# A state space stage on GpSimd: shared first phases, copies moved to ScalarE, a feed-through and an input split moved to VectorE

## The chip, the cores and the metric

The kernel runs on one core of a Trainium2 chip. The core has a matrix engine (TensorE, in the profile PE, with its weight loads as PEld), VectorE (DVE), ScalarE (ACT), GpSimd (POOL) and SyncE (SP), which only issues DMAs. Each engine works through its own list of instructions in order; an instruction that waits holds all behind it on its engine. The metric is device time in microseconds for one execution of the whole program.

## The reference

Two trunk layers are computed for 1024 latent tokens and 128 context tokens (1152 columns in all), D = 1024. Layer 0 mixes tokens by a diagonal state space model (S5) and by differential attention; layer 1 by a short convolution and a gated recurrence. Each is followed by a gated convolutional FFN (D_FF = 2816). What matters here is the S5 part and the product into the second FFN:

```python
def s5_direction(u, lam_re, lam_im, log_dt, b_w, c_w, h0, reverse):
    ...
    ab_r, ab_i = mag * jnp.cos(ang), mag * jnp.sin(ang)
    ...
    if h0 is not None:
        br = br.at[:, 0].add(ab_r * h0r - ab_i * h0i)
        bi = bi.at[:, 0].add(ab_r * h0i + ab_i * h0r)
    _, _, hr, hi = lax.associative_scan(_cplx_comb, (ar, ai, br, bi), axis=1)
    final = jnp.stack([hr[:, -1], hi[:, -1]], axis=1)
    y = jnp.einsum('blgn,gpn->blgp', hr, c_w[0]) - jnp.einsum('blgn,gpn->blgp', hi, c_w[1])
    return y, final

# in mixer_ab: both directions, 32 groups of 16 channels and 64 states
ys = u4 * s5_d.reshape(S5_G, S5_P)          # the feed-through
ys = ys + y_d                                # for d in (forward, backward)
ys = jax.nn.gelu(ys.reshape(b, L, HALF))

def conv_ffn(h, w_up, cw, cb, w_down):
    u = dwconv(h @ w_up, cw, 1) + cb
    g, val = jnp.split(u, 2, axis=-1)
    return (jax.nn.gelu(g) * val) @ w_down
```

## The kernel before

Every large matrix product is done in three: each factor is split into a rounded part (`hi`, written by ScalarE) and the remainder (`lo`, a subtraction on VectorE or GpSimd), and hi·hi, hi·lo and lo·hi are added in PSUM.

**State space stage.** The sequence is cut in chunks of 8 tokens, 144 chunks with both token groups. The 32 groups are done in 8 blocks of 4 (`G_ = 4`); both directions sit in the upper and lower 64 partitions. `s5_params` first works out the parameters of all groups, almost all of it on VectorE; among them `Lr`, `Li`, the phase of one chunk squared 0 to 6 times. Then, for each block, `s5_prep` builds its tables and `s5_main` uses them. The table `E` holds the phases of 0 to 143 chunks, made by doubling: for `m` from 0 to 6 the first `n = 2**m` columns times phase `m` give the next `n`, in six GpSimd instructions (L619 to L621); the last 16 columns repeat the first 16 (L623). `s5_prep` also makes `ca` (GpSimd product `d`, VectorE sum, L655 and L656), the convolution kernel of a chunk (`kps` on TensorE, `ks`, with the feed-through `dd` added on its middle, L673 to L676, written to DRAM as `kt` and read back as `M`, both by DMAs on ScalarE's queue, L677 and L680), and the input matrix `W` (products `d` L685 to L687, transposed as `wps`). `s5_main` multiplies the inputs by `W` (`zps`), turns them by `E` (`x`), scans them on VectorE (`X`, L727 and L728), copies the last states out and the first states in (L731 to L737, GpSimd), turns them back (`s`, GpSimd L743 and VectorE L744 and L745), multiplies by `ca` and `M` (`yps`) and applies the gelu (L758). Table `b + 1` is prepared before block `b` is used. `s5_main` is emitted at higher priority.

**Order.** The instructions' order on each engine comes from a planner that simulates the program as written and lets later work (the projections for attention, `vps` and `pps`, and the modulation rows `mps`) fill time in which earlier work waits. It is fixed before the run.

**Second FFN.** Its up projection runs as a seven-product scheme on 2 by 2 blocks of inputs (`11`, `12`, `21`, `22`, `T1` to `T4`, four slices each of 576 columns). `T1` and `T2` are made as the tokens arrive (`Blocks.put`), the rest in `Blocks.rest`: for each input the rounded part on ScalarE and the remainder on the named engine (`split`, L107 and L108), `T3 = 22 - 12` (L115) and `T4 = 21 - T2` in two subtractions (L122 and L126). The function `after` chains these instructions so that each engine keeps the order in which they are written. The products themselves (`prod`, L1565, result `sps`) come in the order T2, T1, 11, 22, 21, T3, T4, and their weights are split by `pair` (`wp`, L1505 and L1506).

## Time and profile before

| | us |
|---|---|
| median of 3 runs | 2981.25 |
| lowest, highest | 2980.51, 2983.24 |
| the profiled execution | 2977.45 |
| its span, first to last instruction | 2975.7 |

| engine | busy us | share of the span |
|---|---|---|
| PE | 2779.2 | 93% |
| DVE | 2053.7 | 69% |
| ACT | 1136.2 | 38% |
| POOL | 955.6 | 32% |

Busy time is that of instructions on the engine; DMA issues and waits are not in it. The shares are means over stages that differ much. Durations further on come from the profiled execution, whose time stands beside its span above.

### The profile page before, as it was taken

What the parts mean: (1) busy time and instruction counts of PE and PEld (TensorE: products, weight loads), DVE (VectorE), ACT (ScalarE), POOL (GpSimd) and SP (SyncE); (2) the same over time, 40 slices, a digit from 0 to 9 for tenths busy, and PEclk for the clock granted to TensorE, in tenths of its full rate; (3) what the DMA queues carried; (4) which work ended last, traced back from release to release, by engine and by line L of the source; (5) the groups of instructions that cost most, each with busy time, mean ns of one, the idle gap of its engine ahead of it and who ended that gap; (6) DMA issues with size and microseconds to landing.
All of it is one profiled execution on the core that took longest, in us unless ns stands there. A gap on an engine that the chain in (4) does not pass through costs nothing.

```text
span 2975.7 us, 41289 instructions
## 1 busy us (share of the span) xinstructions
PE 2779.2 (93%) x15560; PEld 2504.5 (84%) x15560; DVE 2053.7 (69%) x3266; ACT 1136.2 (38%) x1916; POOL 955.6 (32%) x1047
## 2 busy tenths in 40 slices
PE   7977687998999999999999989999979999998998
PEld 3875566787789999999999979997769999997887
DVE  6767784876468888888655684456488888884224
ACT  5222122776353222222222365564544444443211
POOL 2699972012130000000000251111166666653100
PEclk9988898999999999999999989999979999999999
DMA  6424447334543332333111231124312222225323
GB/s 224 130 64 111 112 132 225 111 98 122 161 141 100 93 100 81 98 100 95 48 43 57 71 116 55 54 94 132 110 46 72 70 84 69 69 96 168 93 61 123
DMA packets 315653, 299.68 MB, mean 101 GB/s; under 512 B 46334, under 2 KB 272338, under 8 KB 315454
## 3 DMA queue, kind: packets, MB, share of 16 engines
q1 hardware_dynamic: 293544, 261.00, 28.5%
q0 software_dynamic: 4496, 20.91, 2.1%
q10 hardware_dynamic: 17414, 15.14, 1.9%
q8 instruction: 122, 2.00, 0.3%
q14 instruction: 77, 0.63, 0.1%
HBM read 230.68 MB, written 66.30 MB: 100 GB/s over the span
## 4 chain that ended last, share of the span: by engine, by line
PE 63%; issue 3%; DVE 2%; POOL 2%; ACT 1%; DMA 0%; ACTq 0%; POOLq 0%; DVEq 0%; SPq 0%
PE pps L189 27%; PE sps L1565 16%; PE dps L189 8%; PE dps L1682 8%; PE ops L189 3%; PE gps L189 1%; POOL hl L54 1%; DVE l L108 0%; DVE yl L1398 0%; POOL rs L239 0%; PE tps L377 0%; POOL tf L115 0%; PE mps L334 0%; PE mps L333 0%; POOL q L239 0%
## 5 line engine op out<-in xcount | busy, mean ns | idle before, releaser
L189 PE MATMUL pps<-hl,whi 128*128 128x384 f32 (+1 forms) x1824 | 624.2, 342 | 1.5 <-DVE hl L886 0.8
L189 PE MATMUL pps<-hh,whi 128*128 128x384 f32 (+1 forms) x1824 | 624.5, 343 | 0.3 <-DVE lruc L1342 0.3
L189 PE MATMUL pps<-hh,wlo 128*128 128x384 f32 (+1 forms) x1824 | 622.4, 342 | 2.3 <-DVE wlo L201 2.3
L189 PEld LDWEIGHTS pps<-hh,whi 128*128 128x128 f32 x1824 | 346.7, 190 | 10.2 <-issue 3.9
L189 PEld LDWEIGHTS pps<-hh,wlo 128*128 128x128 f32 x1824 | 346.6, 190 | 8.5 <-DVE wlo L201 3.2
L189 PEld LDWEIGHTS pps<-hl,whi 128*128 128x128 f32 x1824 | 346.6, 190 | 7.7 <-DVE hl L886 1.6
L201 POOL TENSOR_TENSOR wlo<-wr,whi 128x1024 fp32r<-128x1024 f32 x22 | 57.0, 2603 | 737.8 <-PE dps L189 595.2
L1682 PE MATMUL dps<-wp,wp 128*128 128x512 f32 x1188 | 279.5, 397 | 8.0 <-DVE C L1523 5.9
L1682 PEld LDWEIGHTS dps<-wp,wp 128*128 128x128 f32 x1188 | 225.4, 190 | 62.0 <-ACT cc L1642 6.1
L1639 DVE SCALAR_TENSOR_TENSOR cc<-C,cvc,cc 128x1023 f32<-128x1023 f32 (+1 forms) x176 | 225.8, 1322 | 35.1 <-ACT cc L1634 35.1
L1565 PE MATMUL sps<-h,wp 128*128 128x288 f32 x1056 | 188.7, 298 | 10.7 <-DVE wp L1506 9.4
L1436 DVE SCALAR_TENSOR_TENSOR cc<-pps,cvc,cc 128x384 f32<-128x384 f32 (+2 forms) x352 | 171.1, 509 | 39.8 <-ACT cc L1433 37.7
L326 DVE SCALAR_TENSOR_TENSOR macc<-mw,sil,macc 128x256 f32<-128x256 f32 x392 | 176.1, 484 | 17.9 <-DMA mw<-w_mod 17.1
L1482 DVE TENSOR_TENSOR acc<-acc,dps 128x512 f32<-128x512 f32 x180 | 122.4, 680 | 76.3 <-PE dps L189 75.7
L1565 PEld LDWEIGHTS sps<-h,wp 128*128 128x128 f32 x1056 | 157.8, 190 | 11.2 <-DVE wp L1506 9.6
L199 ACT ACTIVATE whi<-wr 128x1024 fp32r<-128x1024 f32 x102 | 107.5, 1056 | 153.9 <-PE pps L189 101.7
L189 PE MATMUL dps<-whi,mh 128*128 128x512 f32 x396 | 156.9, 397 | 1.2 <-DVE acc L1482 1.2
L189 PE MATMUL dps<-wlo,mh 128*128 128x512 f32 x396 | 156.6, 396 | 0.0
L189 PE MATMUL dps<-whi,ml 128*128 128x512 f32 x396 | 155.6, 393 | 0.0
L1433 ACT ACTIVATE cc<-pps,cvc 128x385 f32<-128x385 f32 (+1 forms) x132 | 87.4, 665 | 173.9 <-PE pps L189 160.9
L201 DVE TENSOR_TENSOR wlo<-wr,whi 128x1024 fp32r<-128x1024 f32 x80 | 101.8, 1274 | 70.8 <-PE pps L189 36.2
L1523 POOL TENSOR_TENSOR C<-U,X 128x576 f32<-128x576 f32 x44 | 105.4, 2396 | 134.2 <-DVE U L1523 134.2
(423 smaller groups left out, 6033.5 us busy)
## 6 DMA issues: line engine op xcount, KB each, us to landing
mw<-w_mod SPq DMA_DIRECT2D x224, 128.0 KB
x<-x SPq DMA_DIRECT2D x45, 512.0 KB
wr<-ffn_w_up SPq DMA_DIRECT2D x44, 512.0 KB
wr<-ffn_w_down SPq DMA_DIRECT2D x44, 512.0 KB
wm<-w_mod SPq DMA_DIRECT2D x40, 512.0 KB
m<-cc SPq DMA_DIRECT2D x21, 576.0 KB
k<-kh POOLq DMA_DIRECT2D x8, 1408.0 KB, 6.7
wv<-ffn_w_up SPq DMA_DIRECT2D x21, 512.0 KB
```

The lines of the kernel that those rows point to most:

```text
L54: nc.gpsimd.tensor_tensor(lv, h, f(hv), op=OP.subtract)
L189: nc.tensor.matmul(ps, x, y, start=first and i == 0 and j == 0, stop=last and i == n - 1 and j == 2)
L199: nc.scalar.activation(hi, raw, AF.Copy)
L201: (eng or nc.vector).tensor_tensor(lo, raw, f(hi), op=OP.subtract)
L326: nc.vector.scalar_tensor_tensor(acc[v], wt, s, acc[v], op0=OP.mult, op1=OP.add)
L1433: nc.scalar.activation(cc[:, :no], ps[:, q:q + no], AF.Identity, bias=cw[3], scale=cw[1])
L1436: nc.vector.scalar_tensor_tensor(cc[:, oa - o0:ob - o0], ps[:, oa + d - i0:ob + d - i0], cw[j], cc[:, oa - o0:ob - o0], op0=OP.mult, op1=O ...
L1482: nc.vector.tensor_tensor(acc[t][:, sl], acc[t][:, sl], ps, op=OP.add)
L1523: tt = lambda e, o, x, y, op: e.tensor_tensor(o, x, y, op=op)
L1565: nc.tensor.matmul(ps[:, c, :W2], w, z[:, c * W2:c * W2 + W2], start=m == 0, stop=m == len(steps) - 1)
L1639: nc.vector.scalar_tensor_tensor(cc[:, o0:o1], src[:, o0 + d:o1 + d], cw[j], cc[:, o0:o1], op0=OP.mult, op1=OP.add)
L1682: nc.tensor.matmul(ps[:, h], mt[:, x, i], W[fb][:, y, h * 512:h * 512 + 512], start=i == 0 and j == 0, stop=i == n - 1 and j == 2)
```

## The change

The first three doublings of `E` (columns 0 to 7) are computed for all 32 groups at once, in `s5_params`, into two tables `EP`; each block copies its part from there on ScalarE and goes on with `m = 3`. The copy of the last 16 columns of `E`, and the four state copies of each scan, go from GpSimd to ScalarE; the two memsets between them stay on GpSimd. The feed-through `dd` on GpSimd and its addition on VectorE become one fused instruction on VectorE for each group. `h0` is kept in a rotating buffer in place of a constant one. In `Blocks.rest` the differences for `T3` and the remainders of `T3` go from GpSimd to VectorE, the `T3` split is put ahead of `T4`, and `T4` is worked slice by slice: both subtractions, the rounding, the remainder.

```diff
@@ Blocks.rest
         for i in range(4):
-            after(G.tensor_tensor(t3[i], raw["22"][i], raw["12"][i], op=OP.subtract))
+            after(V.tensor_tensor(t3[i], raw["22"][i], raw["12"][i], op=OP.subtract))
...
+        self.hi["T3"], self.lo["T3"] = new("T3h"), new("T3l")
+        split("T3", t3, V)
         t4 = temp()
+        self.hi["T4"], self.lo["T4"] = new("T4h"), new("T4l")
         for i in range(4):
             after(V.tensor_tensor(t4[i], raw["21"][i], f(self.hi["T2"][:, i]), op=OP.subtract))
-        self.hi["T3"], self.lo["T3"] = new("T3h"), new("T3l")
-        split("T3", t3, G)
-        for i in range(4):
             after(V.tensor_tensor(t4[i], t4[i], f(self.lo["T2"][:, i]), op=OP.subtract))
-        self.hi["T4"], self.lo["T4"] = new("T4h"), new("T4l")
-        split("T4", t4, V)
+            after(A.activation(self.hi["T4"][:, i], t4[i], AF.Copy))
+            after(V.tensor_tensor(self.lo["T4"][:, i], t4[i], f(self.hi["T4"][:, i]), op=OP.subtract))
@@ s5_params
+        G = nc.gpsimd
+        self.EP = [C([128, 32, 8], f"EP{x}") for x in range(2)]
+        G.memset(self.EP[0][:, :, 0:1], 1.0)
+        G.memset(self.EP[1][:, :, 0:1], 0.0)
+        for m in range(3):
+            n = 1 << m
+            lr, li = (x[:, m, :, None].to_broadcast([128, 32, n]) for x in (self.Lr, self.Li))
+            e0, e1 = (e[:, :, 0:n] for e in self.EP)
+            for o, x0, x1, op in ((0, lr, li, OP.subtract), (1, li, lr, OP.add)):
+                t0, t1 = self.tp([128, 32, n]), self.tp([128, 32, n])
+                G.tensor_tensor(t0, e0, x0, op=OP.mult)
+                G.tensor_tensor(t1, e1, x1, op=OP.mult)
+                G.tensor_tensor(self.EP[o][:, :, n:2 * n], t0, t1, op=op)
...
-        self.h0 = C([128, 2, 32], "h0")
+        self.h0 = self.ST.tile([128, 2, 32], F32, tag=self.STt, name="h0")
@@ s5_prep
-        G.memset(E[0][:, :, 0:1], 1.0)
-        G.memset(E[1][:, :, 0:1], 0.0)
-        for m in range(7):
+        for e, p in zip(E, self.EP):
+            nc.scalar.activation(e[:, :, 0:8], p[:, g0:g0 + G_], AF.Copy)
+        for m in range(3, 7):
...
-            G.tensor_copy(e[:, :, 128:144], e[:, :, 0:16])
+            nc.scalar.activation(e[:, :, 128:144], e[:, :, 0:16], AF.Copy)
...
-            dd = self.small.tile([16, 2, 16], F32, tag="dd", name=self.nm("dd"))
-            G.tensor_tensor(dd, self.eye16[:, None, :].to_broadcast([16, 2, 16]),
-                            self.Dc[:, g0 + hf * 2:g0 + hf * 2 + 2, None].to_broadcast([16, 2, 16]), op=OP.mult)
             V.tensor_tensor(ks[:, :, 7], ks[:, :, 7], kp[1][:, gs, 112:128], op=OP.add)
-            V.tensor_tensor(ks[:, :, 7], ks[:, :, 7], dd, op=OP.add)
+            for i in range(2):
+                g = g0 + hf * 2 + i
+                V.scalar_tensor_tensor(ks[:, i, 7], self.eye16, self.Dc[:, g:g + 1], ks[:, i, 7], op0=OP.mult, op1=OP.add)
@@ s5_main
-            G.tensor_copy(self.fs[up, r, g0:g0 + G_], X[up, 145:145 + 144 * 3 + 1:144])
-            G.tensor_copy(self.fs[lo, r, g0:g0 + G_], X[lo, 128:128 + 144 * 3 + 1:144])
+            nc.scalar.activation(self.fs[up, r, g0:g0 + G_], X[up, 145:145 + 144 * 3 + 1:144], AF.Copy)
+            nc.scalar.activation(self.fs[lo, r, g0:g0 + G_], X[lo, 128:128 + 144 * 3 + 1:144], AF.Copy)
             w = X[:, 1:577].rearrange("q (g c) -> q g c", c=144)
-            G.tensor_copy(w[up, :, 0], self.ini[up, r, g0:g0 + G_])
+            nc.scalar.activation(w[up, :, 0], self.ini[up, r, g0:g0 + G_], AF.Copy)
             G.memset(w[up, :, 128:129], 0.0)
-            G.tensor_copy(w[lo, :, 127], self.ini[lo, r, g0:g0 + G_])
+            nc.scalar.activation(w[lo, :, 127], self.ini[lo, r, g0:g0 + G_], AF.Copy)
             G.memset(w[lo, :, 143:144], 0.0)
```

## Rows read from the trace of the kernel before

**Rows 1.** Busy time by stretch: stretch, length, then each engine (instructions), granted clock, DMA.

```profile
104.00:410.00 306.00, 232.26 (x1451) 195.53 (x1450) 214.58 (x300) 59.65 (x142) 285.28 (x537) 0.88 0.39 103
455.00:516.00 61.00, 49.40 (x230) 38.44 (x229) 23.31 (x25) 13.94 (x21) 14.37 (x10) 0.90 0.73 225
516.00:2155.00 1639.00, 1592.18 (x8432) 1462.94 (x8430) 1148.07 (x1970) 717.59 (x1273) 234.92 (x230) 0.99 0.31 95
2189.00:2199.00 10.00, 0.64 (x4) 0.40 (x3) 10.00 (x9) 1.35 (x2) 7.02 (x4) 0.57 0.00 0
2199.00:2672.00 473.00, 473.00 (x3543) 473.00 (x3543) 404.57 (x409) 196.17 (x255) 298.48 (x165) 0.99 0.23 73
```

**Rows 2.** Instructions in time, POOL, state space stage: start, length, line, idle before.

```profile
103.84 0.23 POOL L673 TENSOR_TENSOR dd<-misc,Dc 16x32 f32<-16x32 f32 x1 [17.21 <-DVE Dc L595]
...
289.13 0.21 POOL L621 TENSOR_TENSOR E<-et,et 128x4 f32<-128x4 f32 x1
...
292.02 0.22 POOL L621 TENSOR_TENSOR E<-et,et 128x16 f32<-128x16 f32 x1
```

**Rows 3.** Instructions of tile `yps`, ns min/median/max, first and last start.

```profile
L758 ACT ACTIVATE u<-yps x16: 398/410/413, 166.9 to 454.0; 128x288 f32<-128x288 f32 x16
```

**Rows 4.** Waits in all, 130 to 440 us: total us, times, longest.

```profile
PE wps L690 <- DVE d L687: 44.3, 9, 8.2
```

**Rows 5.** Instructions in time, PE, start of the second FFN.

```profile
2198.63 1.33 PE L1565 MATMUL sps<-h,wp 128*128 128x288 f32 x4 [9.36 <-DVE wp L1506]
```

**Rows 6.** Instructions in time, DVE, start of the second FFN.

```profile
2176.08 6.03 DVE L108 TENSOR_TENSOR l<-b,h 128x576 fp32r<-128x576 f32 x4 [1.31 <-POOL tf L115]
...
2189.21 7.43 DVE L122 TENSOR_TENSOR tf<-b,T2h 128x576 f32<-128x576 f32 x4
...
2198.50 0.75 DVE L126 TENSOR_TENSOR tf<-tf,T2l 128x576 f32<-128x576 f32 x1
```

**Rows 7.** Instructions in time, POOL, start of the second FFN.

```profile
2168.61 7.44 POOL L115 TENSOR_TENSOR tf<-b,b 128x576 f32<-128x576 f32 x4
...
2186.75 7.54 POOL L108 TENSOR_TENSOR T3l<-tf,T3h 128x576 fp32r<-128x576 f32 x4
...
2215.28 1.30 POOL L1523 TENSOR_TENSOR ws<-wv 128x512 f32<-128x512 f32 x1
```

**Rows 8.** Groups by line and shape, 60 to 460 us: busy us, mean ns, idle before.

```profile
L731 POOL COPY fs<-X 64x4 f32<-64x4 f32 x16 | 11.9, 743 | 5.2 <-DVE X L727 2.6 <-DVE x L724 2.4
L673 POOL TENSOR_TENSOR dd<-misc,Dc 16x32 f32<-16x32 f32 x16 | 8.7, 550 | 18.1 <-DVE Dc L595 17.2 <-DVE d L676 0.7
L621 POOL TENSOR_TENSOR E<-et,et 128x128 f32<-128x128 f32 x16 | 7.6, 474 | 0.6
L623 POOL COPY E<-E 128x64 f32<-128x64 f32 x16 | 6.9, 434 | 0.0
L734 POOL COPY X<-ini 64x4 f32<-64x4 f32 x16 | 5.5, 343 | 0.3
L676 DVE TENSOR_TENSOR d<-d,dd 16x32 f32<-16x32 f32 x16 | 4.8, 302 | 0.2
L621 POOL TENSOR_TENSOR E<-et,et 128x4 f32<-128x4 f32 x16 | 4.6, 287 | 1.2
L619 POOL TENSOR_TENSOR et<-E,Lr 128x8 f32<-128x8 f32 x8 | 1.8, 224 | 0.6
```

**Rows 9.** Instructions of a line, ns min/median/max, first and last start; ACTq is ACT's DMA queue.

```profile
L731 POOL COPY fs<-X x16: 177/676/1306, 153.8 to 440.0; 64x4 f32<-64x4 f32 x16
L680 ACTq DMA_DIRECT2D M<-kt x64: 546/605/686, 131.3 to 416.9; - x64
L677 ACTq EVENT_SEMAPHORE  x16: 17/3146/9960, 120.2 to 405.7; - x16
```

**Rows 10.** Instructions in time, ACT.

```profile
365.43 0.49 ACT L1021 ACTIVATE qr<-pps 128x384 f32<-128x384 f32 x1 [10.73 <-DMA M<-kt]
...
506.36 0.20 ACT L1263 ACTIVATE su<-ones 128x1 f32<-128x1 f32 x1
```

## Prediction

> **What bounds the kernel now.** I read the table of stretches first, then the group table of POOL, then the order of instructions in the two places the diff touches. In the state space stage, from 104 to 410 us, the table of stretches [rows 1] shows POOL busy for 285.3 of 306 us, DVE for 214.6, PE for 232.3 at a granted clock of 0.88, ACT for 59.7. The one idle stretch of POOL that matters lies ahead of it: 17.2 us before the first `dd` [rows 2]. The eight blocks of four groups leave the stage at the pace of their gelu, the first of its 16 evictions at 166.9 us and the last at 454.0 us, seven blocks on: (454.0 - 166.9) / 7 = 41 us a block [rows 3]; POOL's 285.3 us over 7.5 blocks are 38. So the stage runs at POOL's pace, and PE, which fills its gaps with the projections, stands still behind waits for DVE sums that need a POOL product (44.3 us in nine waits of `wps` alone [rows 4]). After the stage come 61 us in which the rest of the Q and K projections runs (PE 49.4 us busy [rows 1]); the softmax can't begin in earnest before these, and from 516 to 2155 us PE is busy for 1592.2 of 1639 us [rows 1]. What is saved before 516 us therefore reaches the end.
>
> In the second FFN, PE computes without a gap from 2199 to 2672 us [rows 1], but ahead of it stands a hole of 9.36 us, in which PE waits for a weight remainder on DVE [rows 5]. That wait is not for the weight: DVE is in the middle of the `T4` differences [rows 6], and POOL beside it computes the remainder of `T3` [rows 7]. The granted clock of 2189 to 2199 us is 0.57 [rows 1], so mostly the lower of its two levels, 1.2 GHz.
>
> **The change, part by part.** *Phases 1, 2 and 4 long, once for all groups.* Removed from POOL in each block: 18 products and sums of 4, 8 and 16 elements. They are 15 groups of shapes, with 45.3 us in all 8 blocks; the costliest and the cheapest stand in [rows 8]. In a quiet run 12 of them take 292.02 - 289.13 = 2.89 us, 0.24 us each with the gaps [rows 2], so 18 x 0.24 x 8 = 35 us unstretched. Two memsets a block go too; I leave them out of the sum. Added once: 18 POOL instructions of 32, 64 and 128 elements. The nearest rows are those of POOL sums of the same sizes, of which 128 elements have a mean of 0.47 us [rows 8]: 18 x 0.47 = 8 us, or 5 by the unstretched price. They need only `Lr`, `Li` of the first three levels, and POOL is idle for 17.2 us there [rows 2]; they are hidden, and cost 5 to 8 us if the planner puts them behind 104 us.
>
> *Small copies to ScalarE.* Removed from POOL: the four state copies of each scan (four groups of 16, 33.4 us in all, the first and the last of them shown), the 16 tail copies `E<-E` (6.9 us), and the 16 `dd` (8.7 us) [rows 8]. The shortest are 0.18 us for a state copy [rows 9] and 0.23 for a `dd` [rows 2], which I take for the tails too: 64 x 0.18 + 32 x 0.23 = 19 us unstretched. Added on ACT: 64 state copies, 16 tails, 16 starts. No row shows a copy of four elements on ACT; the nearest below is 0.20 us for one element, above 0.49 us for 384 [rows 10]: 96 copies are 19 to 47 us, and I take the lower end, which four elements are nearest to. ACT has 306 - 59.7 us not busy, but much of that is taken: the 64 DMA issues `M<-kt` take 0.605 us each (39 us), the waits for `kt<-d` on its queue have a median of 3.1 us and reach 10.0 us [rows 9], and one projection's eviction stood 10.7 us behind them [rows 10]. A state copy that falls in such a stretch holds the block's POOL product `s<-X,E`, and POOL's whole queue behind it: the products of the next block, and so DVE's sums `ca` and `d`, and PE's `kps` and `wps`. A block keeps ACT in issues and waits for some 8 x 0.605 + 2 x 3.1 = 11 us of 41. A scan meets that with a chance of about 0.27, and then waits half of 5 us on the mean; two scans, 8 blocks: 0.27 x 2.5 x 16 = 11 us. The bounds are 0 (the copies fall between) and 8 x 10.7 = 86 us (each block meets the longest). I take 10, since most waits are near the median.
>
> ScalarE: Activation LUTs, section "What ACT_TABLE_LOAD costs", in the Trainium skill, gives 186 ns plus 0.833 ns per element for an activation with immediate scale; by it the 96 copies would be an estimated 19 us, the lower end above. By that page a copy is no shorter on ACT than POOL's shortest, so the move pays only where POOL waits for its turn, not in the copy itself. No trace here shows a four-element ACT copy.
>
> *Feed-through on DVE.* Per block, 2 sums of 32 elements go (mean 0.30 us [rows 8]) and 4 fused multiply-adds of 16 by 16 come, two of them for each sum that goes; at the same price 32 x 0.30 = 9.6 us against 16 x 0.30 = 4.8 us: 5 us more on DVE, hidden in DVE's 91 us not busy, but 5 us on the stage if DVE becomes its bound.
>
> *`h0`* only moves to a rotating buffer; no instruction is added.
>
> *Sum of the stage.* POOL loses 35 + 19 = 54 us by unstretched prices and 45.3 + 33.4 + 6.9 + 8.7 = 94 us by busy time. The stretch is time in which DVE holds what POOL needs, and it moves on to POOL's next instruction; so I take the lower, and 6 us more because `dd` no longer keeps the first block's phases waiting (0 to 12 us: 17.2 less the new 5). That is 60 us. DVE then is the next limit: 214.6 + 5 us in 306 - 60 = 246, 89%. PE would have to do 232 us in 246; I let 8 us of projection go to the tail (bounds: 0, if a higher granted clock pays for it, and 40). Less 10 for ACT: 60 - 10 - 8 = 42 us. Bounds: 54 - 10 - 40 = 4 us, and 91 us, the slack of DVE, which 94 + 12 would pass.
>
> *Second FFN.* The four differences `t3` (7.44 us on POOL) and the four remainders of `T3` (7.54 us) go to DVE [rows 7]. Beside POOL a DVE operation of 576 elements takes 1.86 us (7.43 / 4), with POOL idle 0.75 [rows 6]. DVE's queue grows by 8 x 0.75 = 6 us; the 4 first `T4` differences shrink by 4 x 1.1 = 4.4 us, and the remainders of 11 and 22 by up to 8 x 1.1 = 8.8, since POOL's `t3` no longer meets them. The first products of `22` wait no longer than now: DVE stood waiting 1.31 us for POOL's `t3` ahead of them [rows 6]. Each `T4` slice now waits for ACT's rounding between two DVE operations, some 4 x 0.7 us by DVE's price of the same size. The remainder weight of PE's hole gets 4.4 + 8.8 - 6 = 7 us earlier, and less by what POOL's own weight sums still stretch. I take 6 us. Bounds: 0 (PE meets the next missing piece of `T4`) and 9.4 + 4 (the hole gone, and the halved clock behind it).
>
> SBUF — State Buffer, section "SBUF: two separate sides", in the Trainium skill, says that a GpSimd instruction and a DVE instruction with two inputs in SBUF exclude each other for their whole length. By this rule alone the eight moved operations save an estimated 8 x (1.46 - 0.75) = 5.7 us, with POOL's price of 1.30 us for 512 elements, made up to 576 [rows 7], against the 6 us that I take from the queue. The rows agree with it in part: 1.86 us beside each other is less than the 1.46 + 0.75 of taking turns in full.
>
> The sum: 42 + 6 = 48 us. The profiled execution took 2977.45 us (span 2975.7 us and 1.75 around it): 2929.5. The median of the runs, 2981.25 us, is 3.8 us above it: 2933.
>
> **The rivals.** *ACT becomes the place where blocks wait, slower.* One mechanism: the planner sets a state copy behind `M<-kt`, and every block waits. Without ACT's waits the sum gives 60 - 8 + 6 = 58 us, so it decides from 58 / 8 = 7.3 us a block; at the longest row, 10.7 us, it costs 86 us: 2981 + 86 - 58 = 3009. For it: ACT runs in order, its waits reach 10 us. Against: the median is 3.1 us. 0.09.
>
> *Given back by PE.* The stage gets shorter, but PE at 232 of 306 us is nearly as full as POOL, and the projections that filled the gaps run afterwards: 30 to 40 us go back; 60 - 10 - 35 + 6 = 21, so about 2960. For it: the tail of 61 us holds three of eight Q and K projections already. Against: PE's durations in the stage are those of a 0.88 clock, and waits that hold it go with POOL's load. 0.16.
>
> *All the busy time comes back.* POOL is relieved by 94 us, DVE fills, the clock rises: 70 us or more, 2911 and below, down to 2890. For it: DVE and PE both have over 70 us of slack. Against: DVE would have to be busy for 95% of the stage. 0.13.
>
> *Nothing arrives.* The planner keeps the pace, for instance because the start copies into `E` wait on ACT for the block before to let the buffer go, and POOL waits with them. Within 6 us of 2981. 0.05.
>
> **How the numbers follow.** My case has 0.57, its own range 2918 to 2948. 0.2% of 2981 is 6 us, about what a measurement can tell from none. Faster: 0.57 + 0.16 + 0.13 = 0.86; same 0.05; slower 0.09. The range from 2902 to 2972 leaves out the slower case, the unchanged one and about half of the largest gain, some 0.2.
>
> **What would show it.** In the profile after: POOL in the stage under 85% busy, a pace near 33 to 35 us a block, the softmax beginning 35 to 50 us earlier, the gaps of `wps` smaller. ACT's copies near 0.2 us, without gaps of 5 us ahead of POOL's `s<-X,E`; such gaps would speak for the first rival. PE fuller than 92% in the stage with a tail longer than 61 us: the second. In the second FFN: the hole of 9.36 us under 4 us, DVE's operations there near 0.75 us, the `T4` products at the same distance from the last transpose less 6 us. The prediction fails if the new order on ACT or PE makes other waits than those counted.

## The result and the profile after

The changed kernel takes 2949.89 us (median of 4 runs, 2949.02 to 2954.14) against 2981.82 us for the kernel before on the same chip: ratio 0.9896, 95% interval 0.9879 to 0.9913, some 32 us faster. That is within the range, 17 us longer than the forecast, and just outside the likeliest case's own range. The profiled execution after took 2954.14 us, the longest of the four, and that of before 2977.45 us, below its median; so between the two profiles only 23.3 us are to be found.

They arise in two places. The first attention score, the product of `sA`, starts 17.6 us earlier. First the kernel before, then the changed one (the instructions of the tile: ns min/median/max, first and last start):

```profile
L1136 PE MATMUL sA<-k,q x400: 273/393/796, 504.4 to 706.3; 128*128 128x512 f32 x96, 128*128 128x256 f32 x32, 128*128 128x128 f32 x6
```

```profile
L1149 PE MATMUL sA<-k,q x400: 273/393/793, 486.8 to 689.7; 128*128 128x512 f32 x96, 128*128 128x256 f32 x32, 128*128 128x128 f32 x6
```

From there the lead stays between 16.6 us (the last `sA`) and 18.4 us (the first product of the second FFN, at 2149.81 against 2168.17 us). In the second FFN it grows by 4.7 us: the last product with `T4h` starts at 2655.4 against 2678.5 us.

**The stage.** The table of stretches of the changed kernel (length, then each engine's busy time and instructions, granted clock, DMA) answers to the first line of [rows 1]; the other lines run to the end of the last gelu, from there to the first score, and over both:

```profile
104.00:410.00 306.00, 242.49 (x1500) 199.57 (x1498) 244.38 (x372) 81.77 (x246) 221.97 (x283) 0.88 0.40 105
104.00:428.70 324.70, 257.77 (x1582) 214.21 (x1581) 260.49 (x395) 85.31 (x255) 229.85 (x288) 0.88 0.42 112
428.70:486.80 58.10, 56.66 (x268) 42.21 (x267) 19.97 (x22) 10.29 (x17) 10.66 (x5) 1.00 0.70 213
104.00:486.80 382.80, 314.43 (x1848) 256.42 (x1847) 280.46 (x416) 95.60 (x271) 240.51 (x293) 0.90 0.46 127
```

The kernel before, in the same three stretches:

```profile
104.00:454.40 350.40, 273.04 (x1643) 224.90 (x1642) 254.21 (x352) 70.32 (x162) 306.50 (x558) 0.89 0.39 107
454.40:504.40 50.00, 43.03 (x209) 33.76 (x208) 13.03 (x15) 6.68 (x12) 8.05 (x5) 0.93 0.71 218
104.00:504.40 400.40, 316.07 (x1850) 258.65 (x1849) 267.24 (x366) 77.00 (x173) 314.56 (x562) 0.89 0.43 120
```

POOL (the fifth engine column) falls from 93% of the first 306 us to 73%. The last line of each fence is the one to remember: up to the first score PE has the same work, 1848 and 1850 matmuls and 314.4 and 316.1 us; what changed is the time in which PE does nothing, 400.40 - 316.07 = 84.3 us before and 68.4 us after. These 16 us are the gain of the stage, with 1.6 us of shorter PE time. This is an account and not yet a cause: the first score starts when PE has done this work and stood through its waits.

The blocks' pace, by the gelu as in [rows 3], is (428.3 - 171.9) / 7 = 36.6 us against 41.0; the first gelu comes 5.0 us later, the last 25.7 us earlier:

```profile
L771 ACT ACTIVATE u<-yps x16: 388/410/423, 171.9 to 428.3; 128x288 f32<-128x288 f32 x16
```

PE's waits of the changed kernel up to the first score (us in total, times, longest) answer to [rows 4]. The waits of `wps` for a sum on DVE are the ones that shrank, from 44.3 and 3.5 us for two lines to 15.5 and 11.4 us. The last three lines, waits for ScalarE, are new or longer; before, one of 7.0 us was the only large one:

```profile
PE wps L703 <- DVE d L700: 15.5, 4, 6.1
PE wps L703 <- DVE d L686: 11.4, 3, 6.1
PE yps L769 <- DVE s L758: 10.9, 5, 4.2
PE wps L703 <- ACT v L1012: 7.0, 1, 7.0
PE nkps L1038 <- ACT qr L1034: 5.5, 2, 4.1
PE pps L189 <- ACT qr L1034: 3.7, 2, 3.4
```

```profile
PE mps L296 <- ACT qr L1021: 7.0, 1, 7.0
```

Added up over the whole list, PE's waits for VectorE fall from 76.7 to 49.6 us and those for ScalarE rise from 7.4 to 18.5 us. Together they are PE's idle time to within 0.3 us, before and after.

What POOL has left got longer. Two of its groups after (busy us, mean ns, idle before); in the kernel before, the same 16 products `s<-X,E` took 26.1 us and the same 32 products `d` 29.4 us:

```profile
L756 POOL TENSOR_TENSOR s<-X,E 128x576 f32<-128x576 f32 x16 | 40.5, 2534 | 3.3 <-ACT X L749 2.0 <-POOL X L750 0.8
L669 POOL TENSOR_TENSOR d<-b,PCi 128x320 f32<-128x320 f32 x32 | 35.1, 1119 | 1.4 <-DVE d L700 0.6 <-ACT b L653 0.5 <-DMA kt<-d 0.3
```

And POOL now stands still where it didn't before. Its waits after, 104 to 430 us:

```profile
POOL et L633 <- ACT E L625: 15.7, 5, 6.1
POOL x L732 <- DVE x L729: 12.8, 2, 12.0
POOL b L657 <- DMA b<-s_b: 10.8, 1, 10.8
...
POOL X L748 <- DVE X L740: 7.8, 5, 2.0
...
POOL s L756 <- ACT X L749: 2.0, 3, 0.8
```

**ScalarE's copies** cost what the prediction took: a state copy 0.19 to 0.21 us, against 0.18 us at POOL's best and a median of 0.68 us for the first of the four groups [rows 9]. But each pair of them stands at the head of this engine's queue and waits for the scan, 35.2 and 22.7 us in all for the two `fs` lines (instructions of a line, then ScalarE's waits):

```profile
L744 ACT ACTIVATE fs<-X x16: 207/208/209, 149.3 to 410.1; 64x4 f32<-64x4 f32 x16
...
L749 ACT ACTIVATE X<-ini x16: 205/206/207, 151.2 to 415.2; 64x4 f32<-64x4 f32 x16
```

```profile
ACT fs L744 <- DVE X L740: 35.2, 15, 7.0
...
ACT fs L745 <- DVE X L741: 22.7, 16, 4.4
```

**The second FFN.** The hole of [rows 5] is gone; PE's longest waits between its first product and the steady stretch are now these (instructions in time, idle before in brackets):

```profile
2157.08 0.80 PE L1578 MATMUL sps<-T1h,wp 128*128 128x288 f32 x4 [1.28 <-DVE wp L1519]
...
2165.66 0.54 PE L1578 MATMUL sps<-h,wp 128*128 128x288 f32 x2 [3.00 <-ACT wp L1518]
...
2169.01 1.33 PE L1578 MATMUL sps<-h,wp 128*128 128x288 f32 x4 [0.97 <-POOL wp L1519]
```

On DVE the four `t3` differences and the four remainders of `T3` took 0.96 and 0.69 us each, where POOL took 1.86 and 1.89 [rows 7]; beside POOL's weight sums a remainder of `11` still takes 1.77 on the mean:

```profile
2145.59 7.06 DVE L108 TENSOR_TENSOR l<-b,h 128x576 fp32r<-128x576 f32 x4
2152.58 3.84 DVE L115 TENSOR_TENSOR tf<-b,b 128x576 f32<-128x576 f32 x4
...
2163.79 2.76 DVE L108 TENSOR_TENSOR T3l<-tf,T3h 128x576 fp32r<-128x576 f32 x4
```

Not all of it lasts. From the first product of this FFN to the first with `T4h` takes 33.0 us (2149.8 to 2182.8) where it took 41.4 (2168.2 to 2209.6), 8.4 us less; from there to the last product with `T4h` it takes 472.6 us against 468.9, and in this stretch PE now waits 2.5 us for weight remainders on DVE, where it had no wait.

### The profile page after: what moved, and what is told of

Read it like the earlier page. It is cut to its first block, busy times and chain, and to the rows that moved or that the text cites. A ratio compares the mean times of both kernels' runs of the same rounds, so it can differ in the third digit from the quotient of the medians.

```text
span 2952.3 us, 41202 instructions
## 1 busy us (share of the span) xinstructions
PE 2775.5 (94%) x15560; PEld 2499.6 (85%) x15560; DVE 2066.9 (70%) x3290; ACT 1152.9 (39%) x2012; POOL 874.0 (30%) x803
## 4 chain that ended last, share of the span: by engine, by line
PE 72%; issue 3%; DVE 3%; ACT 2%; DMA 1%; POOL 1%; SPq 0%; DVEq 0%; POOLq 0%; ACTq 0%
PE pps L189 27%; PE sps L1578 15%; PE dps L189 8%; PE dps L1695 8%; PE ops L189 6%; PE sA L1149 3%; PE ops L1225 2%; PE wtp L1181 1%; PE gps L189 1%; DVE cc L1652 1%; PE tps L377 1%; DMA y<-gs 0%; DMA gy<-ys 0%; DVE yl L1411 0%; ACT e L1160 0%
```

## The experiments

Each ratio is to the kernel before on the same chip; by the same comparison the changed kernel stands at 0.9896. The theories are named in the expectations: A, ScalarE's in-order queue holds the pace; B, VectorE's work is the bound; C, the waits follow the order in which the engines were planned; D, one block's chain and its buffers set the pace.

**The stage alone** (the second FFN as before):

```diff
-            after(V.tensor_tensor(t3[i], raw["22"][i], raw["12"][i], op=OP.subtract))
+            after(G.tensor_tensor(t3[i], raw["22"][i], raw["12"][i], op=OP.subtract))
...
-        split("T3", t3, V)
+        split("T3", t3, G)
...
```

> The state space stage as changed, the second FFN's split as before. In the profile of the changed kernel the attention scores begin 17.6 us earlier, and the last products of the second FFN 23.1 us earlier, so 17 to 18 of it arise in the stage and 5 behind it. If the two parts don't touch each other: 27 us faster than before by the medians (31.9 less 4.7), ratio 0.991. If the stage alone gives only the 17.6 us that the scores show: ratio 0.994.

Ratio 0.9919 [0.9906, 0.9933], some 24 us; PE idle up to the first score at 489.1 us: 385.10 - 313.84 = 71.3 us. The time lies between the two figures, nearer to that of parts that don't touch each other.

**The second FFN alone** (the stage as before; the first hunk of the change, of which this is the core):

```diff
-            after(G.tensor_tensor(t3[i], raw["22"][i], raw["12"][i], op=OP.subtract))
+            after(V.tensor_tensor(t3[i], raw["22"][i], raw["12"][i], op=OP.subtract))
...
-        split("T3", t3, G)
+        split("T3", t3, V)
...
+            after(A.activation(self.hi["T4"][:, i], t4[i], AF.Copy))
...
```

> Only the second FFN's split as changed. My theory (the hole ahead of the T4 products closes from 9.36 us to 3 or less, smaller gaps of 1 to 3 us open elsewhere): 4 to 6 us faster, ratio 0.998 to 0.9987. Rival (the hole's place is taken by other late pieces once the stage isn't changed too): within 2 us.

Ratio 0.9988 [0.9979, 0.9997], 3.6 us, between the two expectations and nearer to the first; the interval holds 1 to 6 us. First to last product of the second FFN is 2673.9 - 2166.6 = 507.3 us, against 510.3 before and 505.6 in the changed kernel. The two parts make 0.0081 + 0.0012 = 0.0093 of the changed kernel's 0.0104: they add up within the intervals.

**Phases once and feed-through on VectorE, no copies on ScalarE** (the second FFN as before; lines against the changed kernel, the other three state copies likewise):

```diff
-            nc.scalar.activation(e[:, :, 0:8], p[:, g0:g0 + G_], AF.Copy)
+            G.tensor_copy(e[:, :, 0:8], p[:, g0:g0 + G_])
...
-            nc.scalar.activation(e[:, :, 128:144], e[:, :, 0:16], AF.Copy)
+            G.tensor_copy(e[:, :, 128:144], e[:, :, 0:16])
...
-            nc.scalar.activation(self.fs[up, r, g0:g0 + G_], X[up, 145:145 + 144 * 3 + 1:144], AF.Copy)
+            G.tensor_copy(self.fs[up, r, g0:g0 + G_], X[up, 145:145 + 144 * 3 + 1:144])
...
```

> First phases once for all groups and the feed-through on VectorE; all small copies stay on POOL (the 16 start copies too, in place of ScalarE). POOL loses some 35 us unstretched. Theory A (ScalarE's in-order queue costs much of what the stage could have gained): it gives as much as the whole stage part or more, 20 to 35 us faster, ratio 0.988 to 0.993. Theory B (VectorE and the chain of blocks limit the gain, ScalarE's copies do what they should): 10 to 17 us, ratio 0.994 to 0.997, less than the whole stage part by what the copies bring.

Ratio 0.9954 [0.994, 0.9968], 14 us: theory B's figure. The last gelu starts at 432.8 us, 21.2 us earlier than before, the scores at 495.5 us, 8.9 us earlier.

**The copies alone** (64 state copies and 16 tails on ScalarE, the rest as before):

```diff
-            G.tensor_copy(e[:, :, 128:144], e[:, :, 0:16])
+            nc.scalar.activation(e[:, :, 128:144], e[:, :, 0:16], AF.Copy)
...
-            G.tensor_copy(self.fs[up, r, g0:g0 + G_], X[up, 145:145 + 144 * 3 + 1:144])
+            nc.scalar.activation(self.fs[up, r, g0:g0 + G_], X[up, 145:145 + 144 * 3 + 1:144], AF.Copy)
...
-            G.tensor_copy(w[up, :, 0], self.ini[up, r, g0:g0 + G_])
+            nc.scalar.activation(w[up, :, 0], self.ini[up, r, g0:g0 + G_], AF.Copy)
...
```

> Only the 64 state copies and the 16 tail copies on ScalarE. POOL loses 15 us unstretched, 40 us of busy time. Theory A (ScalarE's in-order queue eats it): within 5 us of before, or slower. Theory B: 8 to 15 us faster, ratio 0.995 to 0.997.

Ratio 0.9988 [0.9979, 0.9997], 3.6 us: theory A's figure. The last gelu starts at 438.4 us, 15.6 us earlier than before, and the scores at 504.9 us, no earlier at all. So the copies did speed up the blocks, and PE gave all of it back: its idle time is 84.6 us, as before, with 10.3 us less of waits for VectorE and 10.6 us more of waits for ScalarE, and the projections left over make the tail from last gelu to first score 66.5 us long, where it was 50.4. ScalarE's own waits show where it stands: the tail copies wait for POOL sixteen times.

```profile
ACT E L623 <- POOL E L621: 51.8, 16, 7.8
ACT fs L731 <- DVE X L727: 34.2, 13, 6.0
```

By the time the two halves bring 14 + 4 us apart and 24 together, about 6 us more than the sum, which is hardly clear of the intervals (some 3 to 4 us each). At the last gelu it is the other way: 21.2 + 15.6 = 36.8 us apart, 25.7 together.

**Start copies on POOL:**

```diff
-            nc.scalar.activation(e[:, :, 0:8], p[:, g0:g0 + G_], AF.Copy)
+            G.tensor_copy(e[:, :, 0:8], p[:, g0:g0 + G_])
```

> The changed kernel with the 16 start copies of E on POOL. It takes away the 15.7 us for which POOL stands waiting for these copies and adds some 4 us to POOL. Theory A (ScalarE's in-order queue holds POOL and so the pace): 5 to 12 us faster than the changed kernel, ratio to before 0.986 to 0.988. Theory B (the pace hangs on VectorE, which POOL's idle time doesn't touch): no different from the changed kernel, ratio 0.989 to 0.9905.

Ratio 0.9916 [0.9903, 0.993]; the last gelu at 437.0 us, 8.7 us later than in the changed kernel, the scores at 486.2 us, 0.6 us earlier. POOL's 15.7 us of waiting for `E` are gone, and nothing is won: theory A falls for this wait, the longest of POOL's after. The ratio is a little above theory B's range too, with an interval that reaches into it. PE's waits for ScalarE fall from 18.5 to 12.2 us, and those for VectorE rise from 49.6 to 58.8.

**Transfers `M<-kt` issued from SyncE:**

```diff
-            nc.scalar.dma_start(M[j * 16:j * 16 + 16], kt[:, :, (7 - j) * 16:(7 - j) * 16 + 128])
+            nc.sync.dma_start(M[j * 16:j * 16 + 16], kt[:, :, (7 - j) * 16:(7 - j) * 16 + 128])
```

> The changed kernel with the 64 transfers M<-kt issued from SyncE, so that ScalarE's queue no longer waits for kt. Theory A: ScalarE's copies and evictions come sooner, 5 to 15 us faster than the changed kernel, ratio 0.985 to 0.988; the PE and POOL waits behind ScalarE shrink. Theory B: no different, 0.989 to 0.9905. A slower run would say that SyncE's queue (weights, state inputs) is held by the wait for kt in its place.

2943.66 us, ratio 0.9883 [0.987, 0.9897]; the scores start at 475.3 us, 11.5 us earlier than in the changed kernel. Its table of stretches up to there:

```profile
104.00:475.30 371.30, 308.21 (x1843) 250.21 (x1842) 279.63 (x410) 95.28 (x271) 237.56 (x293) 0.91 0.47 130
```

PE idle 63.1 us, and 6 us less busy at a granted clock of 0.91. By the profile the issues on ScalarE's queue were a cost; the time, whose interval overlaps that of the changed kernel, shows 4 us of it. It lies between the ranges of A and B and decides neither; PE's waits put down to ScalarE did not shrink (21.7 us against 18.5), those for VectorE did (41.2 against 49.6).

**State copies on VectorE** (all four lines in this way):

```diff
-            nc.scalar.activation(self.fs[up, r, g0:g0 + G_], X[up, 145:145 + 144 * 3 + 1:144], AF.Copy)
+            V.tensor_copy(self.fs[up, r, g0:g0 + G_], X[up, 145:145 + 144 * 3 + 1:144])
...
-            nc.scalar.activation(w[up, :, 0], self.ini[up, r, g0:g0 + G_], AF.Copy)
+            V.tensor_copy(w[up, :, 0], self.ini[up, r, g0:g0 + G_])
```

> The changed kernel with the 64 state copies on VectorE, right behind the scans that they read. ScalarE loses its 57.9 us of waits for scans; VectorE gets 64 x 0.16 = 10 us more. Theory A: 4 to 12 us faster than the changed kernel, ratio 0.986 to 0.9885. Theory B: VectorE is the bound, so 3 to 10 us slower, ratio 0.9905 to 0.993.

Ratio 0.9975 [0.9965, 0.9985], about 24 us slower than the changed kernel, more than either theory allowed; scores at 503.5 us, PE idle 399.50 - 316.38 = 83.1 us. The median copy is as short as expected, the mean isn't. Two of the four lines as instructions (min/median/max), then two of the four as groups (busy us, mean ns):

```profile
L744 DVE COPY fs<-X x16: 149/160/1362, 153.4 to 422.7; 64x4 f32<-64x4 f32 x16
...
L749 DVE COPY X<-ini x16: 168/172/1286, 159.4 to 423.3; 64x4 f32<-64x4 f32 x16
```

```profile
L749 DVE COPY X<-ini 64x4 f32<-64x4 f32 x16 | 8.9, 554 | 0.4
L745 DVE COPY fs<-X 64x4 f32<-64x4 f32 x16 | 7.0, 437 | 0.3
```

The 64 copies hold VectorE for 27.7 us (8.9, 7.0 and, for the other two groups, 6.1 and 5.7), between the scans and the products that the block waits for. One of them, and POOL beside it (start, length): a copy with a median of 0.17 us takes 1.27 us and ends where POOL's product does.

```profile
309.45 1.27 DVE L749 COPY X<-ini 64x4 f32<-64x4 f32 x1
```

```profile
309.30 1.39 POOL L756 TENSOR_TENSOR s<-X,E 128x576 f32<-128x576 f32 x1 [1.06 <-DVE fs L745]
```

**Phases for one block only** (ScalarE's start and tail copies of the other seven blocks go with them; `E` has two buffers of its own, and the pool that held it falls from 6 to 2):

```diff
+        first = b == 0
+        if first:
+            self.E1 = [self.SL.tile([128, G_, 144], F32, tag="E", bufs=2, name=self.nm("E")) for _ in range(2)]
+        E = self.E1
...
-        for m in range(3, 7):
+        for m in range(3, 7) if first else ():
...
```

> The changed kernel with E made for the first block only and used for all eight (this leaves out seven eighths of the E work on POOL, so the values of the other blocks are not those of the reference). POOL loses about 14 us a block, 98 in all, and its waits for start copies. If POOL with its waits still sets the pace: the stage loses 40 us or more, ratio 0.976 or less. If VectorE or PE set it: only the stretch that POOL gave VectorE goes, 10 to 15 us, ratio 0.984 to 0.986; under 0.984 speaks for a share of both.

Ratio 0.9858 [0.9845, 0.9871], some 11 us faster than the changed kernel; scores at 466.3 us. To the last gelu, from there to the scores, and both:

```profile
104.00:394.90 290.90, 240.68 (x1548) 200.33 (x1547) 243.29 (x388) 79.75 (x226) 129.83 (x119) 0.93 0.44 116
394.90:466.30 71.40, 65.02 (x297) 47.44 (x296) 22.91 (x23) 10.65 (x18) 12.62 (x6) 0.95 0.64 199
104.00:466.30 362.30, 305.70 (x1843) 247.77 (x1842) 266.20 (x410) 90.40 (x243) 142.44 (x125) 0.93 0.48 132
```

POOL is busy for 98 us less than in the changed kernel, at 39% of the stretch, and the last gelu comes 33.8 us earlier, the scores 20.5. The time is that of the second case, a stage set by VectorE or PE. VectorE is busy for 14.3 us less than in the changed kernel (280.46 to 266.20), though none of its work was taken away: it fits the stretch that the expectation put at 10 to 15 us. Of the 20.5 us at the scores 11.8 are idle time of PE and 8.7 shorter busy time, at a granted clock of 0.93 against 0.90. With POOL mostly idle PE still stands for 56.6 us, 40.1 of it for VectorE and 16.2 for ScalarE: POOL was a part of the pace, not its bound.

**Feed-through on ScalarE:**

```diff
+            for i in range(2):
+                g = g0 + hf * 2 + i
+                nc.scalar.activation(dd[:, i], self.eye16, AF.Copy, scale=self.Dc[:, g:g + 1])
...
-            for i in range(2):
-                g = g0 + hf * 2 + i
-                V.scalar_tensor_tensor(ks[:, i, 7], self.eye16, self.Dc[:, g:g + 1], ks[:, i, 7], op0=OP.mult, op1=OP.add)
+            V.tensor_tensor(ks[:, :, 7], ks[:, :, 7], dd, op=OP.add)
```

> The changed kernel with the feed-through made by ScalarE (32 products of 16x16, eye times Dc) and added on VectorE by one sum of 16x32 a half, in place of two fused operations. VectorE loses 32 x 0.365 us and gets 16 x 0.17 to 0.30 us: 7 to 9 us less. Theory B (VectorE's work is the price of the stage now: 16 us more of it in the run with the state copies on VectorE brought the scores 17 us later): 7 to 9 us faster than the changed kernel, ratio to before 0.9865 to 0.9873. Theory C (the pace hangs on waits in the order in which the engines were planned, and VectorE's sum has little to do with it): within 4 us of the changed kernel, 0.9883 to 0.991, of either sign.

2953.2 us, ratio 0.9918 [0.9905, 0.9932]: no faster than the changed kernel, so theory B falls as it stood; C's range ends below the ratio too, with an interval that reaches into it. VectorE lost 5.5 us up to the scores (275.0 us) and the scores start 4.9 us earlier, at 481.9; the execution's span is only 0.7 us shorter than the changed kernel's, so the rest was lost again behind the scores. PE's waits for VectorE did fall, from 49.6 to 30.7 us, and those for ScalarE rose from 18.5 to 34.2. So the run does not show that VectorE's work has no price, only that it cost about as much on ScalarE.

**Feed-through on ScalarE and `M<-kt` from SyncE** (the run before, and):

```diff
-            nc.scalar.dma_start(M[j * 16:j * 16 + 16], kt[:, :, (7 - j) * 16:(7 - j) * 16 + 128])
+            nc.sync.dma_start(M[j * 16:j * 16 + 16], kt[:, :, (7 - j) * 16:(7 - j) * 16 + 128])
```

> The run before, with the transfers M<-kt issued from SyncE as well. If the two gains add: theory B 11 to 13 us faster than the changed kernel, ratio 0.985 to 0.986; theory C 0 to 8 us, 0.987 to 0.9896.

2941.32 us (2940.26 to 2941.91), ratio 0.9879 [0.9866, 0.9893]; scores at 473.7 us, PE idle 63.5 us. It beats the kernel before by 35 us and has the lowest ratio of the kernels here that leave no work out; the run with `M<-kt` from SyncE and the next one lie within its interval, and the interval of the changed kernel's 0.9896 overlaps it. The result is in theory C's range and not in B's. The single effects would add up to 0.9905, so they don't add that way either.

**The difference `x2 - x3` on POOL as well:**

```diff
-        V.tensor_tensor(x[2], x[2], x[3], op=OP.subtract)
+        G.tensor_tensor(x[2], x[2], x[3], op=OP.subtract)
```

> The run before, with the difference x2 - x3 of each block on POOL in place of VectorE: VectorE loses 8 x 0.98 us, POOL gets 8 x 1.5 us and stands between the products and the first scan. Theory B: 4 to 8 us faster than the run before. Theory C, or the chain products, sum, scan being what the block waits for: slower than the run before by up to 10 us, since the first scan then waits for POOL twice.

Ratio 0.9889 [0.9875, 0.9902]; last gelu 5.7 us later than in the run before (428.6 against 422.9 us), scores 3.1 us earlier (470.6), PE idle 366.60 - 308.12 = 58.5 us, time the same within the interval, which decides neither expectation. The pace of the blocks and the start of the scores went opposite ways.

**More buffers** (on the kernel with phases for one block only):

```diff
-                self.ST = PT("ST", 5)
+                self.ST = PT("ST", 7)
...
-            zp = [psp.tile([128, 2, 144], F32, tag="z", bufs=3, name=self.nm("zps")) for _ in range(2)]
+            zp = [psp.tile([128, 2, 144], F32, tag="z", bufs=4, name=self.nm("zps")) for _ in range(2)]
...
-            psp = P("psa", 3, space=PSUM)
+            psp = P("psa", 2, space=PSUM)
```

> The kernel with the phases made for one block only (it leaves out seven eighths of the E work, as before), with more buffers for the blocks' own chain: 7 instead of 5 for the tiles R, x, X and s, and 4 instead of 3 PSUM buffers for zps and yps (the projections' own fall from 3 to 2). Theory D (the pace is the length of one block's chain from its first product to its gelu, because the next block's products wait for the buffers that this one holds): the next block's products begin before the gelu of the one before, the pace falls from 32 us to 28 or less, ratio to before 0.982 or less. Theory C (the chain follows the order in which PE and VectorE were planned, and the buffers are not what holds it), or PE, which has some 305 us of work up to the first scores however the blocks run: pace within 1.5 us of 32, ratio 0.984 to 0.9875. A loss would be put down to the projections' two PSUM buffers.

Ratio 0.9926 [0.9912, 0.994]: slower than the same kernel with fewer buffers. In the changed kernel a block has eight products `x` on DVE; all but the first come behind the gelu of the block before, which is at 318.23 and 319.19 us:

```profile
313.34 0.45 DVE L728 TENSOR_TENSOR x<-zps,E 128x288 f32<-128x288 f32 x1
323.27 0.45 DVE L729 TENSOR_TENSOR x<-zps,E 128x288 f32<-128x288 f32 x1
```

With more buffers four of the eight come ahead of it, as D said (the first and the second, then ScalarE's gelu):

```profile
274.76 0.44 DVE L731 TENSOR_TENSOR x<-zps,E 128x288 f32<-128x288 f32 x1
281.56 0.46 DVE L732 TENSOR_TENSOR x<-zps,E 128x288 f32<-128x288 f32 x1 [0.52 <-PE zps L729]
```

```profile
283.03 0.41 ACT L774 ACTIVATE u<-yps 128x288 f32<-128x288 f32 x1 [2.45 <-PE yps L772]
```

The pace falls from 32.1 to (373.6 - 163.3) / 7 = 30.0 us and the last gelu comes 54.7 us earlier than in the changed kernel. The scores, at 487.9 us, come 1.1 us later:

```profile
104.00:374.00 270.00, 216.41 (x1418) 184.27 (x1418) 228.66 (x371) 74.19 (x216) 131.54 (x121) 0.90 0.40 103
374.00:487.90 113.90, 97.18 (x458) 75.31 (x457) 33.87 (x37) 18.23 (x29) 19.85 (x8) 0.96 0.62 180
104.00:487.90 383.90, 313.59 (x1874) 259.58 (x1874) 262.52 (x406) 92.42 (x244) 151.39 (x129) 0.92 0.47 126
```

The pace lies between what D and C expected, and the ratio is above both ranges. The projections that the faster blocks pushed aside run behind them, 114 us of tail against 58, and PE idle is 70.3 us, near the 68.4 of the changed kernel. The expectation put a loss down to the projections' two PSUM buffers; how much of it is theirs, this run can't say.

## Why the prediction was right in sign and wrong in one term

The sign and the order of size were right. The forecast of 48 us came as 31.9 by the medians and as 23.4 in the two profiles: 17.6 of the stage where 42 were forecast, 4.7 of the second FFN where 6, and about 1 us between. That the time lies in the range owes something to the range's width: 2949.89 us is nearer to the 2960 of the rival "given back by PE" than to 2933. Step by step:

- **The bound, and with it the relief term, is the step that failed.** The prediction read "the stage runs at POOL's pace" from POOL's busy time and let each of 60 us taken from POOL come off the stage, less 10 for ScalarE: the last gelu was to come 50 us earlier and came 25.7. Up to the first score POOL lost 314.56 - 240.51 = 74.1 us of busy time, 0.35 us at the last gelu for each. This is no fixed rate: phases and feed-through alone give 0.50 (42.4 us of busy time, 21.2 at the last gelu), the copies alone 0.64 (24.3 and 15.6), and on top of both the phases for one block 0.34 (98.1 and 33.8). POOL held the pace in part, and the parts of its relief overlap there. Busy time was also a poor measure of POOL's work: the same 16 products `s<-X,E` took 26.1 us before and 40.5 after.
- **What PE waits for** is what the runs show in its place. The waits of PE up to the first score, by the engine that the profile names as releaser, and the starts of the last gelu and the first score, in us:

| kernel | last gelu | PE idle | for VectorE | for ScalarE | first score |
|---|---|---|---|---|---|
| before | 454.0 | 84.3 | 76.7 | 7.4 | 504.4 |
| copies alone | 438.4 | 84.6 | 66.4 | 18.0 | 504.9 |
| phases and feed-through | 432.8 | 75.6 | 67.5 | 7.8 | 495.5 |
| changed | 428.3 | 68.4 | 49.6 | 18.5 | 486.8 |
| start copies on POOL | 437.0 | 71.0 | 58.8 | 12.2 | 486.2 |
| state copies on VectorE | 439.5 | 83.1 | 66.1 | 16.8 | 503.5 |
| feed-through on ScalarE | 424.7 | 65.2 | 30.7 | 34.2 | 481.9 |
| `M<-kt` from SyncE | 424.2 | 63.1 | 41.2 | 21.7 | 475.3 |
| both of these | 422.9 | 63.5 | 41.9 | 21.5 | 473.7 |
| `x2 - x3` on POOL too | 428.6 | 58.5 | 35.5 | 23.0 | 470.6 |
| phases for one block | 394.5 | 56.6 | 40.1 | 16.2 | 466.3 |
| more buffers | 373.6 | 70.3 | 34.6 | 33.4 | 487.9 |

- **"I let 8 us of projection go to the tail"** was exact as a term: from last gelu to first score 50.4 us before, 58.5 after. As a picture it was too small. PE's work to the first score is 306 to 318 us in every kernel here, so the start of the scores moves with PE's idle time, and with the clock at which it works. The pace of the blocks isn't the measure: four runs moved the last gelu without the scores, or against them (the copies alone, the start copies on POOL, `x2 - x3` on POOL, more buffers).
- **The rival "given back by PE"** therefore named the right mechanism with a wrong price: the copies alone lose all of 15.6 us to it, the run with more buffers more than all of 20.9 against the same kernel without them.
- **ScalarE's 10 us** were of the right size for another reason, and that is luck. The prediction reasoned from state copies that hold POOL's `s`; they hold it for 2.0 us. PE's waits for ScalarE are what grew, by 11.1 us from before to changed, and by 10.6 and 10.7 us in the two pairs that differ mainly by the copies on ScalarE (before and copies alone, phases and feed-through and changed); in the changed kernel 16.2 of the 18.5 us are waits for evictions of the projections (`v`, `qr`). With the state copies on VectorE 16.8 us of them remain, so they are not the state copies' alone. POOL's 15.7 us behind the start copies, which the prediction put under "nothing arrives", cost nothing that the run without them shows; taking the `M<-kt` issues out of the queue brings the scores 11.5 us earlier. The rival "slower" didn't happen.
- **The first phases once** are hidden as forecast: POOL's 18 operations take 7.1 us and end at 94.4 us, ahead of the stage. No earlier start came of the idle stretch, though: the first gelu is 5.0 us later, where 6 us of head start were counted. POOL then stands 10.8 us for the transfer `b<-s_b`, whose first issue is at 110.0 us where it was at 102.5; the kernel with phases and feed-through has it at 109.5 us, the copies alone at 101.7. Why it comes later was not tested.
- **The feed-through** costs VectorE a median of 0.22 us a piece, a mean of 0.37 with the long ones, 11.7 us against 9.6. Moving it to ScalarE won nothing in time; what it costs on VectorE by itself stays open.
- **The second FFN** went as worked out: the hole of 9.36 us is gone; the waits over 0.5 us between the first product and the steady stretch were 1.59, 1.37 and 9.36 us and are 1.28, 3.00 and 0.97. DVE's operations are near 0.75 us where POOL is quiet, and 4.7 us arrive of 6 (3.6 by the times of the run with this part alone), since 3.7 of 8.4 us are lost again behind the first `T4` product.
- **The signs**: POOL at 73%, under 85%, as said; the pace 36.6 us, not 33 to 35; the scores 17.6 us earlier, not 35 to 50; the waits of `wps` smaller, as said. The sign named for the second rival, PE over 92% busy in the stage and a tail over 61 us, did not show (79% and 58 us), though its mechanism did.

What stays open is what would remove PE's last 60 us. In the changed kernel most of them are waits for VectorE, and work moved from VectorE to ScalarE moved the waits with it; no run here that leaves no work out shortens both. One profile is also a rough measure: the stage alone, with the stage of the changed kernel, has its scores at 489.1 us against 486.8 and its waits at 50.1 and 21.0 us; the second FFN alone, with the stage of before, at 505.6 against 504.4 us and 71.6 and 11.6 us. So differences of some 2 us in the scores, or 5 us in a column of waits, say little. Each small edit also gave PE's and VectorE's instructions another order, and differences within the intervals, such as the 6 us by which the kernels with the start copies on POOL and with the feed-through on ScalarE stand behind the changed one, or the 4 us that SyncE's issues won, can be the order's. Theory D's buffers were tried only together with fewer PSUM buffers for the projections and with work left out, so what they do alone is open.

## What to carry to other kernels

Where a filler (here the projections) runs in the gaps of a stage, the gain of a faster stage is read from the idle time of the engine that carries the filler up to the first instruction behind both, and from what it waits for, not from the pace of the stage or from the busiest engine. An engine that is 93% busy with instructions that run longer than in quiet isn't shown to be the bound; a kernel that leaves most of its work out tells in one run how much of the time goes with it. What a us of relief is worth can fall as more is relieved (0.50 and 0.64 for the parts, 0.35 together). Before moving small work to an engine, look at whether its price there is constant (ScalarE here) or has a tail (VectorE beside POOL here).

## What the runs showed of the hardware

The price of a copy of four elements depended on the engine more than expected: on ScalarE 0.19 to 0.21 us in all 64, on VectorE 0.14 to 1.42 us, on POOL 0.18 to 1.31 [rows 9]. In the changed kernel VectorE's products with an operand in PSUM never stretch, and sums of tiles in SBUF do, beside a busy POOL (instructions of a line: ns min/median/max):

```profile
L728 DVE TENSOR_TENSOR x<-zps,E x16: 439/446/458, 141.6 to 399.1; 128x288 f32<-128x288 f32 x16
...
L758 DVE TENSOR_TENSOR s<-s,s x16: 739/908/2934, 163.7 to 423.8; 128x576 f32<-128x576 f32 x16
```

SBUF — State Buffer, section "SBUF: two separate sides", in the Trainium skill, says that a VectorE instruction in a two-port mode, or with two inputs in SBUF beside a GpSimd instruction that reads SBUF, and the GpSimd instruction shut each other out for their whole length. The rows agree for the sums, with 2.93 us for a sum of 0.74, and with none of it where an input is in PSUM. For the copies they agree in what is seen: 1.27 us for a copy of 0.17 that ends with POOL's product; in which mode the copy ran, no row shows. Taken seriously, this makes VectorE and POOL one resource for such work. It would explain why less than a us came of each us taken off POOL, but no run here tested that by itself.
